# Token mixing on other buffers and engines, and a last norm in another order: one change to a two-block kernel on one core

## The chip, the cores and the metric

The kernel runs on one core of a Trainium2 chip. Its time is the device time of one execution in microseconds (us). Lower is better. The engines are named as in the profile: PE is TensorE (PEld its weight loads), DVE is VectorE, ACT is ScalarE, POOL is GpSimd, SP is SyncE, which issues the DMAs.

## The reference

Two transformer blocks on 256 tokens of width 1024, all in float32. The first has two gated feed-forward layers and, between them, a token mixing layer. The second has attention, a recurrence and a large expert layer, and ends in a layer norm. What the change touches of it:

```python
# token mixing: one projection, two recurrences, one output projection
p = y @ w_in
mq, mk, mv, mo, mif, hq, hf, hi, hg = jnp.split(p, PROJ_IDX, axis=-1)
qk = jax.nn.silu(causal_dwconv(jnp.concatenate([mq, mk], axis=-1), conv_w, conv_b))
hm = merge_heads(mlstm_chunkwise(q, k, v, log_i, log_f))      # gates from mif, values mv
ho = merge_heads(hgrn2_chunkwise(hq_, hk_, hv_, hlf))         # decay from hf, values hi
merged = jnp.concatenate([out_m, out_h], axis=-1).astype(y.dtype)
return merged @ w_out

# the end of the second block
x = _layer_norm(DN_ALPHA * x + _peer(x, ...), ln2_g[l], ln2_b[l])
# _layer_norm: mu = mean(x); var = mean((x - mu)**2); (x - mu) * rsqrt(var + eps) * g + b
```

## The kernel before, in words

Each matrix product is made of three matmuls (`mm3`, lines 276 to 278): weights and activations are split into a high and a low part, and high times high, low times high and high times low are added up. The weights come by DMA from SP's queue, one megabyte or so at a time, into two places that take turns. `split` (lines 264 and 265) makes the high part `wh` on ACT and the low part `wl` on DVE (in some stages on POOL).

A scheduler orders each engine's instructions when the kernel is built, by its own estimates of what is ready when. After that each engine runs its list strictly in order and waits wherever an operand is late. So the lists that it made are what the change is read from.

The mixing layer (`mixer`, from line 558) goes in this order:

- `proj_b` projects the channels that are needed with channels on the partitions (tile `pb`): the decay `hs`, the query `hq`, the convolution's inputs `xq`, and at last the gate rows `gi`.
- `proj_a` projects the values with tokens on the partitions (tile `pa`), in eight steps s of two token halves b, 24 matmuls each: `hv` for s 0 and 1, `mv` for 2 and 3, `hg` for 4 and 5, `mo` for 6 and 7. Each half goes to a PSUM buffer that ACT (or DVE) must empty before it can be written again. The PSUM buffers have three tags: `gu` (2 buffers), `ps` (2) and `acc` (4). `pa` takes `gu`.
- The gate rows (lines 593 to 603) are a chain of small steps on DVE and ACT. PE turns two of the rows (`gm`, line 607) and spreads a third over the partitions (`Mb`, lines 617 to 620), and ACT makes the weights `E` from it.
- The convolution (line 732, 24 steps on DVE) fills `y`, and its sigmoid is three passes of ACT over all of `y` (exp, ln, exp: lines 295 to 297) and one product on DVE (line 735).
- The second recurrence works in nine levels L = 0, 1, 2, 4, ... 128 (lines 655 to 688). A level takes exp of the decay sums `P` and `S` on ACT (lines 662 and 667), multiplies by `hq` and `hk` on DVE (663 and 668), takes products on PE (`lv`, line 678), puts them under a mask into `att` on DVE (680), and, for the next level, widens the sums `S` and `P` (671 and 672).
- Then `S`, `num` (the first recurrence's products, lines 740 to 747) and `ho` (777 and 778) on PE. `num` and `ho` share the tag `acc`. ACT takes squares of both and scales them into `mg` (766 and 784), and `hg` and `mo` multiply that.

The lists of PE put the `pa` matmuls between all these, so that PE has work while it would wait.

The last norm (`finish`) has two token halves b. `centred` adds x and the accumulated `acc` (line 1240, sums on the side), makes minus the mean (1243, 1244), and then the sum of squares: on ACT for b = 0, on DVE for b = 1 (1247). `finish` then scales, a quarter of it on ACT and POOL (1303 to 1305), the rest on DVE (1307, 1308), and SP stores each half row as it is done (1309).

Of the kernel before, what the change touches and what calls it, by code (L numbers as in the profile page):

```python
# [7 lines left out]
F32 = mybir.dt.float32  # L8
# [7 lines left out]
AF = mybir.ActivationFunctionType  # L16
OP = mybir.AluOpType
# [4 lines left out]
D = 1024  # L22
# [150 lines left out]
class K:  # L173
# [368 lines left out]
            for f in fill.get(s, ()):  # L542
                f()

    def proj_a(self, src, s, yh, yl, take):
        w = self.weights(src[s], 2048)
        for b in range(2):
            p = self.psum("pa", tag="gu")
            for k in range(KT):
                wh, wl = w[k // 4]  # L550
                t = slice(b * 128, (b + 1) * 128)
                o = slice((k % 4) * 256, (k % 4) * 256 + 256)
                self.mm3(p[:, :256], yh[:, k, t], yl[:, k, t], wh[:, o], wl[:, o], k == 0, k == KT - 1)
            take(b, p[:, :256])

    def mixer(self, yh, yl, fill):
        nc, A = self.nc, self.A
        act, dve = nc.scalar.activation, nc.vector
        with ExitStack() as ctx:
# [8 lines left out]
            y = mx.tile([128, 8, T], F32, name="y")  # L568
# [23 lines left out]
            m = F  # L592
# [11 lines left out]
            p = self.psum("gm", tag="ps")  # L604
# [9 lines left out]
            for h in range(4):  # L614
                p = self.psum("Mb", tag="ps")
# [25 lines left out]
            hk, P, S = big("hk"), big("P"), big("S")  # L641
            for n in range(4):
                i = slice(n * 256, (n + 1) * 256)
# [11 lines left out]
            for n, L in enumerate((0, 1, 2, 4, 8, 16, 32, 64, 128)):  # L655
                if L == 0:
                    a, b = hq, hk
                else:
                    g = 1024 // (2 * L)
                    half = lambda x, i: x.rearrange("p (g two l) -> p g two l", g=g, two=2)[:, :, i]  # L660
                    a, b = qt[n % 2], kt[n % 2]
                    act(half(a, 1), half(P, 1), AF.Exp)
                    dve.tensor_tensor(half(a, 1), half(a, 1), half(hq, 1), op=OP.mult)
                    if L == 1:
                        b = hk
                    else:
                        act(half(b, 0), half(S, 0), AF.Exp)
                        dve.tensor_tensor(half(b, 0), half(b, 0), half(hk, 0), op=OP.mult)
                    if L < 128:
                        end = lambda i: half(P, i)[:, :, L - 1:L].to_broadcast([128, g, L])  # L670
                        nc.gpsimd.tensor_tensor(half(S, 0), half(S, 0), end(1), op=OP.add)
                        nc.gpsimd.tensor_tensor(half(P, 1), half(P, 1), end(0), op=OP.add)
                if L < 128:
                    for bl in range(2):
                        p = self.psum("lv", tag="ps")
                        for h in range(4):
                            o = h * 256 + bl * 128
                            nc.tensor.matmul(p[:, h * 128:(h + 1) * 128], b[:, o:o + 128], a[:, o:o + 128],
                                             start=True, stop=True)
                        dve.copy_predicated(att[:, bl], lev[:, None, n * 128:(n + 1) * 128].to_broadcast([128, 4, 128]),  # L680
                                            p.rearrange("p (h t) -> p h t", h=4))
                else:
                    p = self.psum("lv", tag="ps")
                    for h in range(4):
                        o = h * 256
                        nc.tensor.matmul(p[:, h * 128:(h + 1) * 128], b[:, o:o + 128], a[:, o + 128:o + 256],
                                         start=True, stop=True)
                    act(cross.rearrange("p h t -> p (h t)"), p, AF.Copy)
# [11 lines left out]
            def values(s):  # L700
                o = (s % 2) * 256

                def take(b, p):
                    if s < 2:
                        act(hv[:, b, o:o + 256], p, AF.Copy)
                    elif s < 4:
                        act(mv[:, b, 2 * (s % 2):2 * (s % 2) + 2, :128], p.rearrange("p (h e) -> p h e", h=2), AF.Copy)
                    elif s < 6:
                        dve.tensor_copy(hg[:, b, o:o + 256], p)
                        act(hgs[:, b, o:o + 256], p, AF.Exp, scale=-1.0)  # L710
                        self.sigmoid_of_exp(hgs[:, b, o:o + 256])
                        t = mg[:, b, 512 + o:768 + o]
                        dve.tensor_tensor(t, t, hg[:, b, o:o + 256], op=OP.mult)
                        dve.tensor_tensor(t, t, hgs[:, b, o:o + 256], op=OP.mult)
                    else:
                        act(mo[:, b, o:o + 256], p, AF.Exp, scale=-1.0)
                        self.sigmoid_of_exp(mo[:, b, o:o + 256])
                        t = mg[:, b, o:o + 256]
                        dve.tensor_tensor(t, t, mo[:, b, o:o + 256], op=OP.mult)

                self.proj_a(A["wina"], s, yh, yl, take)
                for f in fill.get(s, ()):
                    f()

            for s in range(4):
                values(s)
# [4 lines left out]
                for j in range(3):  # L731
                    dve.scalar_tensor_tensor(y[:, n], xq[:, n, j:j + 256], w(j), y[:, n], op0=OP.mult, op1=OP.add)
            ysig = mx.tile([128, 8, 259], F32, name="ysig", tag="xq")[:, :, :T]
            self.sigmoid(ysig, y)
            dve.tensor_tensor(y, y, ysig, op=OP.mult)
            num = [[self.psum(f"num{b}{j}", tag="acc", bufs=4) for j in range(2)] for b in range(2)]
            for h in range(4):
                E = Es[h]
                p = self.psum("S", tag="ps")
# [4 lines left out]
                o = slice((h % 2) * 129, (h % 2) * 129 + 129)  # L744
# [5 lines left out]
            for b in range(2):  # L750
                for j in range(2):
                    v = num[b][j][:, :258].rearrange("p (h e) -> p h e", h=2)
                    act(den[:, 4 * b + 2 * j:4 * b + 2 * j + 2], v[:, :, 128], AF.Abs)
                    for h in range(2):
                        i = 4 * b + 2 * j + h
# [7 lines left out]
            for b in range(2):  # L763
                for h in range(4):
                    o = (h % 2) * 129
                    act(mg[:, b, h * 128:(h + 1) * 128], num[b][h // 2][:, o:o + 128], AF.Copy,
                        scale=fac[:, 4 * b + h:4 * b + h + 1])
# [5 lines left out]
            for b in range(2):  # L773
                for h in range(4):
                    o = ho[b][:, h * 128:(h + 1) * 128]
# [6 lines left out]
            for b in range(2):  # L782
                for h in range(4):
                    act(mg[:, b, 512 + h * 128:640 + h * 128], ho[b][:, h * 128:(h + 1) * 128], AF.Copy,
                        scale=fac[:, 4 * b + h:4 * b + h + 1])

            for s in range(4, 8):
                values(s)
# [501 lines left out]
    def finish(self, wk, acc, out):  # L1290
        dve = self.nc.vector
        g, s = self.row(wk, 2), self.row(wk, 3)
        z = self.work.tile([128, 2, D], F32, name="xn", bufs=1)
        for b in range(2):
            mu, r = self.centred(b, acc, z)
            for h in range(2):
                o = slice(h * 512, (h + 1) * 512)
                x, y = self.x[:, b, o], z[:, b, o]
                if h and not b:

                    m = self.small.tile([128, 1], F32, name="lnm")
                    dve.tensor_tensor(m, mu, r, op=OP.mult)
                    self.nc.scalar.activation(y, y, AF.Identity, scale=r, bias=m)
                    self.nc.gpsimd.tensor_tensor(y, y, g[:, o], op=OP.mult)
                    self.nc.gpsimd.tensor_tensor(x, y, s[:, o], op=OP.add)
                else:
                    dve.scalar_tensor_tensor(y, y, mu, g[:, o], op0=OP.add, op1=OP.mult)
                    dve.scalar_tensor_tensor(x, y, r, s[:, o], op0=OP.mult, op1=OP.add)
                self.nc.sync.dma_start(out[0, b * 128:(b + 1) * 128, o], x)


    def top16(self, pool, val, idx, src, n):
# [374 lines left out]
```

## Time and profile before

| what | value |
|---|---|
| median of 3 runs | 1757.65 us (1756.09 to 1761.62) |
| the profiled execution: its own time, its span | 1756.9 us, 1754.9 us |
| busy share of PE, DVE, ACT, POOL | 96%, 66%, 52%, 17% |
| mean granted TensorE clock | 0.985 of full speed |
| the mixing layer, first `pb` to last `pa` matmul | about 240 to 383 us |
| the last norm, from PE's last matmul to the span's end | 1743 to 1755 us |

The span runs from the first to the last instruction of the trace, and the execution's own time is 2.0 us more. The lists of instructions give start, duration, engine, line, operation and tiles; a bracket at the end is idle time of the engine just before it and what ended that. Matmuls overlap in a pipeline, so their pace is read from start to start, not from their durations. The granted clock is 1.00 at 2.4 GHz and 0.50 at 1.2 GHz; a figure between is a mean over a stretch that has both.

### The profile page before, as it was taken

The numbers are of one execution on the slowest core, as the hardware profiler recorded it, in microseconds if no ns is written. First come the engines' busy times: TensorE is split into PE (matmuls) and PEld (weight loads), VectorE is DVE, ScalarE is ACT, GpSimd is POOL, SyncE is SP. The second block draws the span as 40 slices with busy tenths as digits, with TensorE's granted clock in tenths as the row PEclk, the third lists the DMA queues.
The fourth block names the chain that finished last, engine by engine and source line by source line (L and its number), as shares of the span: only waits on it lengthen the run. The fifth ranks groups of instructions, "written<-read, shape, count | busy, mean of one in ns | idle before, by whom it ended". The sixth has DMA issues, their size and how long they took to land.

```text
span 1754.9 us, 30914 instructions
## 1 busy us (share of the span) xinstructions
PE 1688.1 (96%) x12658; PEld 1536.6 (88%) x12658; DVE 1161.0 (66%) x2057; ACT 910.8 (52%) x1424; POOL 305.7 (17%) x183
## 2 busy tenths in 40 slices
PE   3999999999999998999999999999999999999997
PEld 3899988898999997878889999999888888888886
DVE  8887668778655458344377869998556555655555
ACT  4544376376444457334445445887545444555453
POOL 2000011300000132311005600001322223322321
PEclk8999999999999999999999999999999999999998
DMA  8888433357553231401253567877866666777652
GB/s 326 356 342 332 169 129 113 156 218 312 217 202 130 96 117 53 169 31 63 97 186 132 200 227 251 314 299 294 289 242 244 228 245 218 252 248 257 229 202 84
DMA packets 85677, 362.68 MB, mean 207 GB/s; under 512 B 6432, under 2 KB 39328, under 8 KB 52768
## 3 DMA queue, kind: packets, MB, share of 16 engines
q1 hardware_dynamic: 85536, 360.71, 55.7%
q8 instruction: 99, 1.62, 0.4%
q14 instruction: 42, 0.34, 0.1%
HBM read 333.42 MB, written 27.26 MB: 206 GB/s over the span
## 4 chain that ended last, share of the span: by engine, by line
PE 48%; DVE 10%; issue 1%; DMA 1%; ACT 1%; POOL 0%; DVEq 0%; SPq 0%; ACTq 0%
PE acc L276 7%; PE acc L278 7%; PE acc L277 7%; PE pu L276 5%; PE pu L278 4%; PE pu L277 4%; DVE wl L265 3%; DVE dif L1509 2%; DVE oj L1517 1%; PE pg L276 1%; PE pb L276 1%; PE pb L278 1%; PE pb L277 1%; PE pg L278 1%; PE pg L277 1%
## 5 line engine op out<-in xcount | busy, mean ns | idle before, releaser
L264 ACT ACTIVATE wh<-w 128x1024 fp32r<-128x1024 f32 x402 | 422.6, 1054 | 261.5 <-PE acc L277 110.5
L265 DVE TENSOR_TENSOR wl<-w,wh 128x1024 fp32r<-128x1024 f32 x301 | 371.3, 1238 | 222.1 <-ACT wh L264 216.0
L265 POOL TENSOR_TENSOR wl<-w,wh 128x1024 fp32r<-128x1024 f32 x101 | 246.6, 2442 | 1044.9 <-ACT wh L264 892.0
L276 PE MATMUL pu<-yh,wl 128*128 128x256 f32 x1024 | 292.4, 286 | 0.0
L278 PE MATMUL pu<-yl,wh 128*128 128x256 f32 x1024 | 289.4, 283 | 0.0
L277 PE MATMUL pu<-yh,wh 128*128 128x256 f32 x1024 | 288.6, 282 | 0.0
L276 PE MATMUL acc<-wh,gl 128*128 128x512 f32 x512 | 202.2, 395 | 1.2 <-DVE gl L1609 1.1
L278 PE MATMUL acc<-wl,gh 128*128 128x512 f32 x512 | 202.0, 395 | 0.0
L277 PE MATMUL acc<-wh,gh 128*128 128x512 f32 x512 | 202.0, 395 | 0.0
L277 PEld LDWEIGHTS pu<-yh,wh 128*128 128x128 f32 x1024 | 193.6, 189 | 1.2
L276 PEld LDWEIGHTS pu<-yh,wl 128*128 128x128 f32 x1024 | 193.4, 189 | 1.2
L278 PEld LDWEIGHTS pu<-yl,wh 128*128 128x128 f32 x1024 | 193.1, 189 | 0.0
L278 PE MATMUL gu<-yl,wh 128*128 128x256 f32 x416 | 118.2, 284 | 0.0
L277 PE MATMUL gu<-yh,wh 128*128 128x256 f32 x416 | 117.6, 283 | 0.0
L276 PE MATMUL gu<-yh,wl 128*128 128x256 f32 x416 | 117.4, 282 | 0.0
L276 PEld LDWEIGHTS acc<-wh,gl 128*128 128x128 f32 x512 | 96.4, 188 | 23.2 <-DVE gl L1609 2.1
L278 PEld LDWEIGHTS acc<-wl,gh 128*128 128x128 f32 x512 | 96.5, 188 | 22.6
L277 PEld LDWEIGHTS acc<-wh,gh 128*128 128x128 f32 x512 | 96.4, 188 | 21.4
L276 PE MATMUL pb<-yh,wl 128*128 128x256 f32 (+1 forms) x384 | 110.2, 288 | 0.0
L1605 DVE TENSOR_TENSOR H<-H,gate 128x256 f32<-128x256 f32 x128 | 59.7, 505 | 74.8 <-ACT H L1583 71.6
L278 PE MATMUL pb<-yl,wh 128*128 128x256 f32 (+1 forms) x384 | 108.2, 284 | 0.0
L277 PE MATMUL pb<-yh,wh 128*128 128x256 f32 (+1 forms) x384 | 107.5, 283 | 0.0
(511 smaller groups left out, 3799.6 us busy)
## 6 DMA issues: line engine op xcount, KB each, us to landing
w<-in_pu_dram SPq DMA_DIRECT2D x64, 1024.0 KB, 5.4
w<-in_pv_dram SPq DMA_DIRECT2D x64, 1024.0 KB, 4.9
wx<-in_ffn_dram SPq DMA_DIRECT2D x28, 1536.0 KB, 8.8
wa<-in_ada_dram SPq DMA_DIRECT2D x28, 1024.0 KB, 6.2
w<-in_ffn_dram SPq DMA_DIRECT2D x16, 1536.0 KB, 8.9
gd<-gst SPq DMA_DIRECT2D x8, 2048.0 KB, 8.9
gate<-gd SPq DMA_DIRECT2D x32, 512.0 KB, 6.6
hd<-hs SPq DMA_DIRECT2D x36, 256.0 KB, 5.6
```

Source lines behind the costliest of these rows:

```text
L264: nc.scalar.activation(h[:, :n], w, AF.Copy)
L265: eng.tensor_tensor(l[:, :n], w, h[:, :n], op=OP.subtract)
L276: mm(out, ll, rh, start=first, stop=False, **kw)
L277: mm(out, lh, rh, start=False, stop=False, **kw)
L278: self.mm = mm(out, lh, rl, start=False, stop=last, **kw)
L1509: dve.tensor_tensor(d, ix[:, None, None, :].to_broadcast([128, 2, 8, 64]), ij[:, :, t, None].to_broadcast([128, 2, 8, 64]), op=OP.bitwise_xor)
L1517: self.oj = dve.tensor_tensor(oj.rearrange("p m t j -> p (m t j)").bitcast(U32).rearrange("p (m t j) -> p m t j", m=2, t=8), eq.bitcast(U3 ...
L1605: dve.tensor_tensor(g3, g3, gates[m // 2][:, :, 2 * (m % 2) + i], op=OP.mult)
```

## The change

Four things change. The values of s 0 to 3 go to the tag `acc` with its four buffers. The decay sums (671, 672) are issued on DVE. The convolution's sigmoid and product are made in four pieces of two channel groups. The last norm takes its squares on ACT for both halves, multiplies by the weight row ahead of the deviation into a tile of its own (`yfin`), and leaves POOL out.

```diff
-    def proj_a(self, src, s, yh, yl, take):
+    def proj_a(self, src, s, yh, yl, take, tag="gu"):
         w = self.weights(src[s], 2048)
         for b in range(2):
-            p = self.psum("pa", tag="gu")
+            p = self.psum("pa", tag=tag, bufs=4 if tag == "acc" else 2)
...
                     if L < 128:
                         end = lambda i: half(P, i)[:, :, L - 1:L].to_broadcast([128, g, L])
-                        nc.gpsimd.tensor_tensor(half(S, 0), half(S, 0), end(1), op=OP.add)
-                        nc.gpsimd.tensor_tensor(half(P, 1), half(P, 1), end(0), op=OP.add)
+                        dve.tensor_tensor(half(S, 0), half(S, 0), end(1), op=OP.add)
+                        dve.tensor_tensor(half(P, 1), half(P, 1), end(0), op=OP.add)
...
-                self.proj_a(A["wina"], s, yh, yl, take)
+                self.proj_a(A["wina"], s, yh, yl, take, "acc" if s < 4 else "gu")
...
-            self.sigmoid(ysig, y)
-            dve.tensor_tensor(y, y, ysig, op=OP.mult)
+            for n in range(0, 8, 2):
+                i = slice(n, n + 2)
+                self.sigmoid(ysig[:, i], y[:, i])
+                dve.tensor_tensor(y[:, i], y[:, i], ysig[:, i], op=OP.mult)
...
         z = self.work.tile([128, 2, D], F32, name="xn", bufs=1)
+        y = self.work.tile([128, 2, D], F32, name="yfin", tag="yh", bufs=1)
+        half = lambda h: slice(h * 512, (h + 1) * 512)
         for b in range(2):
-            mu, r = self.centred(b, acc, z)
...
+            self.ss(z[:, b], st[:, 3:4], bias=mu)
+            self.rstd(r, st[:, 3:4], D, self.lneps)
+            for h in range(2):
+                dve.scalar_tensor_tensor(y[:, b, half(h)], z[:, b, half(h)], mu, g[:, half(h)], op0=OP.add, op1=OP.mult)
+            for h in range(2):
+                x = self.x[:, b, half(h)]
+                dve.scalar_tensor_tensor(x, y[:, b, half(h)], r, s[:, half(h)], op0=OP.mult, op1=OP.add)
+                self.nc.sync.dma_start(out[0, b * 128:(b + 1) * 128, half(h)], x)
```

All engines' lists differ in the mixing layer and in the last norm, and nowhere else. Lines after 733 are two higher in the new kernel, those after the last norm five. Three places follow.

DVE, the gate rows' chain from the copy of `gi` to the row that PE turns (line 601), before:

```order
L583 COPY gi<-pb 4x512
L594 TENSOR_SCALAR gi<-gi,cols 4x256
L595 TENSOR_SCALAR gi<-gi,cols 4x256
L596 SCALAR_TENSOR_TENSOR rows<-gi 4x256
L265 TENSOR_TENSOR wl<-w,wh 128x1024
L735 TENSOR_TENSOR y<-y,ysig 128x2048
L599 SCALAR_TENSOR_TENSOR gi<-gi,rows 4x256
L265 TENSOR_TENSOR wl<-w,wh 128x1024
L600 SCALAR_TENSOR_TENSOR rows<-rows,gi 4x256
L265 TENSOR_TENSOR wl<-w,wh 128x1024
L601 TENSOR_TENSOR gi<-gi,rows 4x256
```

The same chain in the new kernel (line 737 was 735):

```order
L583 COPY gi<-pb 4x512
L737 TENSOR_TENSOR y<-y,ysig 128x512
L594 TENSOR_SCALAR gi<-gi,cols 4x256
L595 TENSOR_SCALAR gi<-gi,cols 4x256
L265 TENSOR_TENSOR wl<-w,wh 128x1024
L596 SCALAR_TENSOR_TENSOR rows<-gi 4x256
L737 TENSOR_TENSOR y<-y,ysig 128x512 x2
L599 SCALAR_TENSOR_TENSOR gi<-gi,rows 4x256
L600 SCALAR_TENSOR_TENSOR rows<-rows,gi 4x256
L265 TENSOR_TENSOR wl<-w,wh 128x1024
L601 TENSOR_TENSOR gi<-gi,rows 4x256
```

Three of the four pieces of the product stand in it, and two splits of weights in place of three. On PE's list the first `gm` stands behind 64 `pa` matmuls now, and stood behind 86.

PE, from the third `Mb` block to the first levels, in the new kernel:

```order
L617 MATMUL Mb<-rows,ident 128x256
L618 MATMUL Mb<-upper,ident 128x128
L619 MATMUL Mb<-rows,ident 128x128
L620 MATMUL Mb<-upper,ident 128x128
L678 MATMUL lv<-hq,hk 128x128 x8
L678 MATMUL lv<-qt_2952,hk 128x128 x4
L278 MATMUL pa<-wl,yh 128x256
L276 MATMUL pa<-wh,yl 128x256
L277 MATMUL pa<-wh,yh 128x256
L278 MATMUL pa<-wl,yh 128x256
```

Before, the four `Mb` blocks had 8 `pa` matmuls between them, and 4 stood between the first two levels; now the blocks have 1, and 8 stand in the middle of the second level. From level 8 on, 25 or 26 stand between any two levels, where there were 6 to 14.

DVE, one level's work (L = 16), before:

```order
L663 TENSOR_TENSOR qt_2952<-qt_2952,hq 128x32x16
L668 TENSOR_TENSOR kt_2954<-kt_2954,hk 128x32x16
L680 COPY_PREDICATED att<-lev,lv 128x512
L336 SCALAR_TENSOR_TENSOR wa,mod<-wa,sc 128x1024
L680 COPY_PREDICATED att<-lev,lv 128x512 x2
L663 TENSOR_TENSOR qt_2951<-qt_2951,hq 128x16x32
```

And in the new kernel (`wa` is a column product for a later layer, which moved behind the levels):

```order
L663 TENSOR_TENSOR qt_2952<-qt_2952,hq 128x32x16
L668 TENSOR_TENSOR kt_2954<-kt_2954,hk 128x32x16
L671 TENSOR_TENSOR S<-S,P 128x32x16
L265 TENSOR_TENSOR wl<-w,wh 128x1024
L672 TENSOR_TENSOR P<-P 128x32x16
L680 COPY_PREDICATED att<-lev,lv 128x512 x2
L663 TENSOR_TENSOR qt_2951<-qt_2951,hq 128x16x32
```

The two sums stand in DVE's list, with a split between them, ahead of the copies under the mask.

## Rows read from the trace of the kernel before

**Rows 1.** The page's first part: busy time, share and count of each engine.

```profile
PE 1688.1 (96%) x12658; PEld 1536.6 (88%) x12658; DVE 1161.0 (66%) x2057; ACT 910.8 (52%) x1424; POOL 305.7 (17%) x183
```

**Rows 2.** PE's waits, 240 to 420 us: who for, sum us, times, longest.

```profile
PE pa L276 <- ACT hv L705: 3.4, 1, 3.4
PE lv L678 <- DVE att L680: 2.4, 1, 2.4
...
PE lv L678 <- DVE kt L668: 0.8, 2, 0.5
PE ho L778 <- ACT xn L766: 0.3, 1, 0.3
```

**Rows 3.** Instructions of PE in order, 290 to 304 us: start, duration, what.

```profile
292.00 0.28 PE L276 MATMUL pa<-wh,yl 128*128 128x256 f32 x1
...
297.57 0.28 PE L278 MATMUL pa<-wl,yh 128*128 128x256 f32 x1
301.20 0.39 PE L276 MATMUL pa<-wh,yl 128*128 128x256 f32 x1 [3.35 <-ACT hv L705]
...
303.12 0.41 PE L277 MATMUL pa<-wh,yh 128*128 128x256 f32 x1
303.33 0.41 PE L278 MATMUL pa<-wl,yh 128*128 128x256 f32 x1
```

**Rows 4.** Instructions of ACT in order, 290 to 306 us.

```profile
293.65 1.92 ACT L295 ACTIVATE ysig<-y 128x2048 f32<-128x2048 f32 x1 [4.84 <-DVE y L732]
...
300.80 0.36 ACT L705 ACTIVATE hv<-pa 128x256 f32<-128x256 f32 x1
```

**Rows 5.** Instructions of DVE in order, 290 to 308 us.

```profile
293.48 0.67 DVE L583 COPY gi<-pb 4x512 f32<-4x512 f32 x1
...
298.51 1.22 DVE L265 TENSOR_TENSOR wl<-w,wh 128x1024 fp32r<-128x1024 f32 x1 [3.27 <-ACT wh L264]
...
306.02 0.41 DVE L601 TENSOR_TENSOR gi<-gi,rows 4x256 f32<-4x256 f32 x1
```

**Rows 6.** Instructions of PE in order, 310 to 342 us.

```profile
312.75 0.69 PE L617 MATMUL Mb<-rows,ident 4*128 4x256 f32 x2
...
314.86 0.76 PE L617 MATMUL Mb<-rows,ident 4*128 4x256 f32 x2
...
317.59 3.62 PE L678 MATMUL lv<-hq,hk 128*128 128x128 f32 x16
...
338.71 2.02 PE L678 MATMUL lv<-qt,kt 128*128 128x128 f32 x16 [0.53 <-DVE kt L668]
```

**Rows 7.** A stretch: PE, PEld, DVE, ACT, POOL busy, granted clock, DMA share, GB/s.

```profile
315.00:320.00 5.00, 5.00 (x20) 4.15 (x21) 2.74 (x4) 1.47 (x5) 0.11 (x1) 0.54 0.17 69
```

**Rows 8.** Instructions of DVE in order, 330 to 344 us.

```profile
331.29 0.69 DVE L663 TENSOR_TENSOR qt<-qt,hq 128x512 f32<-128x512 f32 x1
331.90 0.69 DVE L668 TENSOR_TENSOR kt<-kt,hk 128x512 f32<-128x512 f32 x1
...
341.40 2.08 DVE L265 TENSOR_TENSOR wl<-w,wh 128x1024 fp32r<-128x1024 f32 x1
```

**Rows 9.** Line 672: engine, count, minimum/median/maximum ns, first and last start.

```profile
L672 POOL TENSOR_TENSOR P<-P x7: 1366/1708/1972, 262.6 to 342.5; 128x512 f32<-128x512 f32 x7
```

**Rows 10.** Instructions of DVE and ACT in order, last norm.

```profile
1741.43 0.16 DVE L1243 TENSOR_TENSOR lnst<-lnst 128x1 f32<-128x1 f32 x1
...
1741.82 1.15 ACT L366 ACTIVATE junk<-xn,lnst 128x1024 bf16<-128x1024 f32 x1 [11.38 <-DVE lnst L1244]
...
1743.42 0.20 ACT L308 ACTIVATE lnst<-lnst 128x1 f32<-128x1 f32 x1
...
1745.41 1.22 DVE L1243 TENSOR_TENSOR lnst<-lnst 128x1 f32<-128x1 f32 x1
...
1746.85 2.18 DVE L1247 SCALAR_TENSOR_TENSOR junkv<-xn,lnst 128x1024 f32<-128x1024 f32 x1
...
1750.40 1.41 DVE L1308 SCALAR_TENSOR_TENSOR x<-xn,lnst,row 128x512 f32<-128x512 f32 x2
```

More of the change, by code (lines that the diff above doesn't have):

```diff
@@ L1293, in finish @@
         z = self.work.tile([128, 2, D], F32, name="xn", bufs=1)
+        y = self.work.tile([128, 2, D], F32, name="yfin", tag="yh", bufs=1)
+        half = lambda h: slice(h * 512, (h + 1) * 512)
         for b in range(2):
-            mu, r = self.centred(b, acc, z)
+            st = self.small.tile([128, 5], F32, name="lnst")
             for h in range(2):
[L1297 to L1309, printed above, removed]
+                dve.scalar_tensor_tensor(z[:, b, half(h)], self.x[:, b, half(h)], 2.0 ** 0.25, acc[b][h], op0=OP.mult,
+                                         op1=OP.add, accum_out=st[:, h:h + 1])
+            mu, r = st[:, 2:3], st[:, 4:5]
+            dve.tensor_tensor(mu, st[:, 0:1], st[:, 1:2], op=OP.add)
+            i = dve.tensor_scalar(mu, mu, -1.0 / D, None, op0=OP.mult)
+            self.ss(z[:, b], st[:, 3:4], bias=mu)
[6 more added lines that the diff above has]
+                self.nc.sync.dma_start(out[0, b * 128:(b + 1) * 128, half(h)], x)
     def top16(self, pool, val, idx, src, n):
```

## The prediction

> **What bounds the kernel now.** The page's first part comes first: PE is busy for 96% of the span, the next engine for 66% [rows 1]. PE's matmuls do not change, so the change can only take out time in which PE waits or runs slowly, and the end behind PE's last matmul. All of that is small: 1% is 17.6 us.
>
> Next come PE's own waits in the mixing layer. Four kinds bear on the change, 6.9 us in all: 3.4 for the eviction of `hv`, 2.4 for a copy under the mask, 0.8 for `kt`, 0.3 for the scaling ahead of `ho` [rows 2].
>
> PE's list around the longest wait shows what it costs. The first 48 `pa` matmuls start 0.119 us apart (292.00 to 297.57 is 47 steps), then PE stands for 3.35 us, and behind it matmuls start 0.21 apart [rows 3]. That is the pace of the lower granted clock, 1.2 GHz. The neighbouring list of ACT says why PE stood: ACT was in the convolution's sigmoid, three passes of 1.92 us, and came to `hv` at 300.80 [rows 4]. Both `gu` buffers were full until then.
>
> A second slow stretch has no wait in front of it. From 315 to 320 us PE is busy all the time, at a granted clock of 0.54 [rows 7]. Ahead of it lie the `Mb` blocks. The first level's sixteen `lv` records span 3.62 us there, against 2.02 at full clock, and a block of `Mb` goes from 2.11 us (two `pa` among it) to 2.73 [rows 6].
>
> The last view is the end of the trace. There DVE alone sets the time: it takes a step of 0.16 us in 1.22 while POOL works, and the squares of b = 1 in 2.18 [rows 10].
>
> **The change part by part.**
>
> *Values in four buffers, sigmoid in pieces.* Removed: the wait of 3.35 us, and the slow pace behind it, some 15 steps of 0.213 - 0.119, 1.4 us [rows 3]. Together 4.75. In the new order PE goes through 64 `pa` matmuls before it needs anything else, from 292.0 to 299.6. Then it needs the gate row of line 601, which came at 306.4 before [rows 5]. So the next late thing is that chain. Its rows by the new list, from a copy of `gi` at about 293: the copy 0.67, three pieces of the product at 0.61 (a product of that size starts 0.61 before the next [rows 8]), four small steps at 0.41, a scan at about 0.6, two splits at 1.22 [rows 5], line 601 itself 0.41: 7.6 us, so 300.6. The 3.27 us that DVE stood behind the split of weights, itself behind ACT's long passes, go away: ACT was idle for 4.84 us before its first pass because the whole of `y` had to be ready [rows 4], and a piece needs only two of the eight groups. I take a wait of 1.0. Its bounds: 0, where the chain is as quick as PE's 64 matmuls, and 6.8, where it comes no earlier than before. Term: -4.75 + 1.0 = -3.75.
>
> ACT's pieces cost it more. From 0.36 us for 256 columns and 1.92 for 2048 [rows 4], 512 columns are about 0.58, twelve of them 7.0 against 5.8. This lies in the 4.84 idle, and if that cover were gone the 1.2 us would go onto the chain, inside the bound above.
>
> *The slow stretch at `Mb`.* Before, it cost 0.86 in the last block (2.73 against 2.11 less two `pa`), 1.6 in the first level, and 0.4 in four `pa`: 2.8 us [rows 3, 6]. The new order packs the blocks closer, one `pa` between them in place of eight, and puts one and a half levels behind them before the next `pa`. I take 1.6 for the first level, 1.2 for most of the second, 0.75 for eight `pa`: 3.6. Term: +0.8. Bounds: -2.8, where the clock stays up, and about +5, where it stays down until the third level has ended.
>
> *Decay sums on DVE.* Removed: the waits at the levels, 2.4 + 0.8 = 3.2 us [rows 2]. The 2.4 came from a split of weights that took 2.08 us in place of 1.22, while POOL was in a sum [rows 5, 8]. Added: nine sums on DVE behind 292 us, five ahead of it. No row has such a sum on DVE. The nearest is the product of the same size, 0.61 from start to start; the far end is POOL's own 1.71 [rows 8, 9]. I take 0.61, since it is the same engine and shape. A level is then, in DVE's list, two products, two sums, two copies under the mask at about 0.61 and a split at 1.22: 4.9 us. PE has 25 `pa` and one level of about 1.9 to do in that time, with the change from one to the other about 5.15. So PE stays behind DVE, barely, and the waits shrink to some 0.5 in all. Term: -2.7. Bounds: -3.2, and up to about +7 with sums at POOL's price (rival C).
>
> The trace has a split beside POOL's work at 2.08 us, and alone at 1.22 [rows 5, 8]: 0.86 lost for one of POOL's sums. The Trainium skill, Perfetto Trace Analysis, section on optimizing Scalar/DVE operations, warns that DVE and GpSimd share a read port, so moving work between the two might not help. Read that way, DVE would pay 0.61 for what it lost before, and the term would be near 0 and the sum 2.7 worse; I keep the term, because PE's waits at the levels came from few such clashes.
>
> *Between the levels and the end of the layer.* Here the order gives back a little. With 46 more `pa` done by then, the first recurrence's `num` comes sooner behind DVE's products with `E`: about 0.5 of waiting. `ho` needs a buffer that `num` leaves once ACT has scaled it, and the squares ahead of that now share ACT with two splits and pieces of `hg`: I take a wait of 1.3 where it was 0.3 [rows 2]. Term: +1.5. Bounds: 0 to +3.
>
> *The last norm.* From 1741.82, when ACT starts the squares of b = 0, DVE has six passes of 512 columns: two products by the weight row, the sum of the first half of b = 1, two last steps of b = 0, the sum of the second half. At 0.70 each (1.41 for two) that is 1746.0; two small steps, 0.4 (1741.43 to 1741.82), 1746.4; ACT's squares and the deviation, 1.8 (1741.82 to 1743.62), 1748.2, with the next two products beside them; two last steps 1.4: 1749.6. Before, the last step ended at 1751.81 [rows 10]. Term: -2.2. Bounds: -2.6 and -1.2, as DVE meets the square later or sooner; the store at the end is the same.
>
> The sum: -3.75 + 0.8 - 2.7 + 1.5 - 2.2 = -6.35 us. From the profiled execution's 1756.9 that is 1750.55. The median of the runs lies 0.75 above that execution, so the forecast for a median is **1751.3**, with its own range of 1749 to 1754.
>
> **The rivals.**
>
> *A, the clock stays up.* PE's slow pace behind the wait goes with the wait, and if the slow stretch at `Mb` is a late effect of the same wait, it goes too. For it: both lie in one stretch of 25 us, and elsewhere the clock is mostly whole. Against it: from 305 to 315 the pace was whole again, and no wait comes before 315 [rows 2, 7]. Worth 0.8 + 2.8: 1747.7. The Trainium skill, TensorE: Matmul & The Clock Gate, on the clock gate, has the clock fall after idling and rise with activity. The first fall agrees with that, the second, with PE busy 5.00 of 5.00, does not.
>
> *B, the wait moves to the gate rows.* DVE has the sums as well now, and the chain stands behind splits that wait for DMA and ACT. If it comes at 303.6, PE waits 4.0 in place of 1.0: 1754.3. For it: every one of its steps waits for another engine or stands in a full list. Against it: the 3.27 idle is gone in any reading.
>
> *C, DVE becomes the bound in the levels: slower.* If a sum costs DVE what it costs POOL, 1.71, a level is 7.1 us against PE's 5.15, and five levels lose 9.75; the five early sums put 5.5 onto the gate rows' chain. 1751.3 + 15.25 is about 1766. The point where the change gains nothing: 15 times the extra per sum, less the 1.25 of slack, is 6.35, at 1.1 us a sum. Against it: the same engine does a product of that shape in 0.69.
>
> *D, only the last norm gains.* PE saves its waits early, meets `num`, `ho` or the clock instead, and the layer ends when it did: 1757.65 - 2.2 = 1755.5. For it: two thirds of the sum rest on waits that come and go with the order.
>
> **How the numbers follow.** 0.3% is 5.3 us, about what a measurement of this kernel can tell from no change, so faster means below 1752.4. The forecast has 0.52 (0.42 below that line, 0.10 above), A 0.14, B 0.16, D 0.11, C 0.07. Faster is 0.42 + 0.14 = 0.56, the same 0.10 + 0.16 + 0.11 = 0.37, slower 0.07. The range of 1746.5 to 1756.5 takes in A, B and D with about 1 us around them and leaves out C and the far ends of the bounds.
>
> **What would show it.** In the new profile `pa` no longer waits for `hv`, and the product of line 737 starts before 295. The first `gm` starts at 300 to 301; a start past 303 is rival B. The granted clock between 306 and 320 decides between A and the forecast. The sums on DVE (lines 671, 672) have a median near 0.69; at 1.1 or more the forecast is wrong. `lv` waits sum to under 1 us. The first `ho` starts near 362, and the last `pa` near 378 in place of 383; 382 is rival D. In the last norm the squares of b = 1 stand on ACT at 1.15, no small step of DVE takes over 0.3, and the last step ends some 6.3 us after PE's last matmul (1743.3 before) in place of 8.5.

## The result, and the profile after

The changed kernel takes **1739.17 us** (median of 6 runs, 1736.62 to 1740.86) against 1759.63 for the kernel before: a ratio of 0.9882, 95% interval 0.9868 to 0.9895. Faster was forecast, but 1751.3 was the forecast and 1746.5 the lower end. The gain is three times the one forecast.

The profiled execution spans 1738.9 us, 16.0 less than before; it was the slowest of its six runs, so the traces show less than the medians. The starts of the same instructions in the two traces show where it comes from. A third column is experiment e1 below, the changed kernel with the SBUF addresses of the kernel before.

| start, us | before | after | e1 |
|---|---|---|---|
| first `gu` (first feed-forward layer) | 52.08 | 51.87 | 51.94 |
| first `pb` (mixing layer) | 239.87 | 237.95 | 239.75 |
| first `pa` | 292.00 | 288.91 | 291.55 |
| last `pa` of the layer | 382.51 | 375.19 | 375.96 |
| `sq` (start of the second block's recurrence) | 652.56 | 642.90 | 646.10 |
| first `pu` (expert layer) | 980.88 | 970.25 | 976.04 |
| last `acc` | 1743.06 | 1729.43 | 1738.84 |
| end of the span | 1754.9 | 1738.9 | 1748.3 |

Between the last `pa` and `sq` neither kernel has another list, and yet the changed one gains 2.3 us more there; in e1 the distance to before changes by 0.1. It gains 1.7 on the way from the first `gu` to the first `pb`, ahead of every edit.

The groups of PE's matmuls by line and shape (busy time, mean ns of one) say what is quicker. Before:

```profile
L276 PE MATMUL pu<-yh,wl 128*128 128x256 f32 x1024 | 292.4, 286 | 0.0
L277 PE MATMUL gu<-yh,wh 128*128 128x256 f32 x416 | 117.6, 283 | 0.0
L277 PE MATMUL gu<-yh,whx 128*128 128x256 f32 x240 | 67.8, 282 | 0.0
```

After:

```profile
L276 PE MATMUL pu<-yh,wl 128*128 128x256 f32 x1024 | 289.7, 283 | 0.0
L277 PE MATMUL gu<-yh,wh 128*128 128x256 f32 x416 | 116.3, 280 | 0.0
L277 PE MATMUL gu<-yh,whx 128*128 128x256 f32 x240 | 67.9, 283 | 0.0
```

The same matmul takes 3 ns less where `yh` streams against `wh` or `wl`, and nothing less where it streams against `whx`, a second place for split weights in the feed-forward layers. How many matmuls fit into a stretch without waits, in the first feed-forward layer, says the same. The columns are those of [rows 7]; the first bracket counts PE's matmuls. Before:

```profile
60.00:160.00 100.00, 100.00 (x700) 93.66 (x699) 82.29 (x123) 45.02 (x60) 0.00 (x0) 1.00 0.85 336
```

After:

```profile
60.00:160.00 100.00, 100.00 (x710) 93.63 (x709) 83.15 (x125) 45.73 (x60) 0.00 (x0) 1.00 0.84 335
```

Ten matmuls more in 100 us, at full clock, with PE busy throughout in both.

Where the change was made, the profile after answers like this. PE's waits from 240 to 420 us, in place of [rows 2]:

```profile
PE gm L607 <- issue: 1.7, 1, 1.7
PE tp L436 <- DVE diag L375: 1.2, 1, 1.2
```

The waits for `hv`, the levels and `ho` are gone, 6.9 us, and one for the gate row (`gm`) has come. "issue" means that the profile names no engine for it; the row comes from DVE's line 601, which ends at 298.22. PE's list shows the wait, and behind it the `Mb` blocks and the first level at half pace, where [rows 6] had one block and the level so:

```profile
296.36 0.28 PE L276 MATMUL pa<-wh,yl 128*128 128x256 f32 x1
298.32 0.25 PE L607 MATMUL gm<-ident,gi 4*128 4x4 f32 x2 [1.68 <-issue]
...
310.43 1.22 PE L617 MATMUL Mb<-rows,ident 4*128 4x256 f32 x2
...
313.61 3.62 PE L678 MATMUL lv<-hq,hk 128*128 128x128 f32 x16
```

The granted clock of that stretch, as [rows 7]:

```profile
302.00:316.00 14.00, 14.00 (x44) 10.00 (x44) 0.61 (x2) 3.14 (x9) 0.11 (x1) 0.50 0.35 148
```

The sums of line 672 on DVE, in place of [rows 9]:

```profile
L672 DVE TENSOR_TENSOR P<-P x7: 666/686/704, 259.5 to 342.2; 128x512 f32<-128x512 f32 x7
```

And the last norm's end on DVE, in place of [rows 10]; PE's last matmul ends at 1729.83:

```profile
1732.16 0.16 DVE L1304 TENSOR_TENSOR lnst<-lnst 128x1 f32<-128x1 f32 x1
...
1732.55 1.42 DVE L1310 SCALAR_TENSOR_TENSOR yfin<-xn,lnst,row 128x512 f32<-128x512 f32 x2
1734.38 1.42 DVE L1313 SCALAR_TENSOR_TENSOR x<-yfin,lnst,row 128x512 f32<-128x512 f32 x2 [0.42 <-ACT lnst L308]
```

No small step takes 1.22 us any more, and the last one ends 6.0 us behind PE (1735.80 less 1729.83), against 8.4 before.

### The profile page after: what moved, and what is told of

Read it like the earlier page. It is cut to its first block, busy times and chain, and to the rows that moved or that the text cites. A ratio compares the mean times of both kernels' runs of the same rounds, so it can differ in the third digit from the quotient of the medians.

```text
span 1738.9 us, 30896 instructions
## 1 busy us (share of the span) xinstructions
PE 1680.8 (97%) x12658; PEld 1526.3 (88%) x12658; DVE 1161.8 (67%) x2073; ACT 912.6 (52%) x1434; POOL 283.2 (16%) x167
## 4 chain that ended last, share of the span: by engine, by line
PE 82%; DVE 12%; ACT 3%; DMA 2%; issue 2%; POOL 0%; SPq 0%; DVEq 0%; ACTq 0%; POOLq 0%
PE acc L276 10%; PE acc L277 10%; PE acc L278 10%; PE pu L276 5%; PE pu L277 5%; PE pu L278 5%; PE gu L276 4%; PE gu L277 4%; PE gu L278 4%; DVE wl L265 3%; PE pb L276 2%; PE pb L278 2%; PE pb L277 2%; DVE dif L1514 1%; PE pg L276 1%
```

## The experiments

The old last norm had a small tile `lnm`, in three slots of 32 bytes per partition. The new one has none. The tiles are laid out one after the other, so every tile behind these slots starts 96 bytes lower in the changed kernel: `yh` and `yl` at 114272 and 106080 in place of 114368 and 106176, and `whx` with them. `wh` and `wl` lie ahead of the slots and did not move. That is the one difference that reaches the untouched layers. Ratios below are to the kernel before, timed on the same chip.

**e1: the old addresses back.**

```diff
+        self.small.tile([128, 24], F32, name="pad", bufs=1)     # never read or written
```

> The changed kernel with 96 unused bytes per partition put back where the old last norm had its three slots of lnm, so that every tile behind them, yh and yl among them, has its old SBUF address; every engine's list is that of the changed kernel. Theory 1 (addresses): TensorE's pace in the layers that the change does not touch depends on where yh and yl lie against wh and wl; then pu<-yh,wl has a mean of about 286 ns again (283 in the changed kernel), and the time is some 9 to 14 us above the changed kernel's 1739.2: 1748 to 1753. Rival (the pace is a matter of the execution or the chip, or comes from the new order): 283 ns stays and the time is 1737 to 1741.

Measured: 1749.84 us, ratio 0.9941 (0.9928 to 0.9953). The group of `pu` in line 276:

```profile
L276 PE MATMUL pu<-yh,wl 128*128 128x256 f32 x1024 | 293.2, 286 | 0.0
```

The stretch of the first feed-forward layer:

```profile
60.00:160.00 100.00, 100.00 (x700) 93.64 (x699) 82.25 (x123) 44.87 (x60) 0.00 (x0) 1.00 0.84 335
```

286 ns and 700 matmuls again. With an order that is not touched, 96 unused bytes cost 10.7 us by the medians. In the mixing layer PE's waits, 240 to 420 us, are these:

```profile
PE tp L436 <- DVE diag L375: 1.2, 1, 1.2
PE gm L607 <- issue: 1.1, 1, 1.1
```

**e2: the new addresses for the kernel before.**

```diff
-        st = self.small.tile([128, 5], F32, name="lnst")
+        st = self.small.tile([128, 6], F32, name="lnst")
...
-        return mu, r
+        self.lm = st[:, 5:6]; return mu, r
...
-                    m = self.small.tile([128, 1], F32, name="lnm")
+                    m = self.lm
```

> The kernel before with lnm kept in a free column of lnst, so that 96 bytes per partition go and every tile behind them has the address that it has in the changed kernel; every engine's list is that of the kernel before. Theory 1 (addresses): pu<-yh,wl falls from 286 to 283 ns and the time from 1759.6 to 1746 to 1751. Rival (execution, chip or order): 286 ns and 1757 to 1762.

Measured: 1750.21 us, ratio 0.9942 (0.9930 to 0.9955). The same group:

```profile
L276 PE MATMUL pu<-yh,wl 128*128 128x256 f32 x1024 | 289.7, 283 | 0.0
```

And the same stretch:

```profile
60.00:160.00 100.00, 100.00 (x710) 93.60 (x709) 83.18 (x125) 45.78 (x60) 0.00 (x0) 1.00 0.85 335
```

The kernel before gains 0.58% by the bytes alone. Half of the result comes from the places of tiles, which moved because the new last norm has no `lnm`, and not from what the four edits do.

**e3 and e4: other distances.** The changed kernel with less padding than e1.

```diff
+e3:     self.small.tile([128, 8], F32, name="pad", bufs=1)
+e4:     self.small.tile([128, 16], F32, name="pad", bufs=1)
```

> The changed kernel with 32 unused bytes: yh, yl and what lies behind them are 64 bytes below their old address, in place of 96. Theory 1a (what counts is whether moving and stationary operand start at the same place modulo 64 bytes): like e1, 1748 to 1753. Theory 1b (modulo 128 bytes): like the changed kernel, 1737 to 1741. Rival (addresses do not matter): 1737 to 1741 here and in e1.

> The changed kernel with 64 unused bytes: yh, yl and what lies behind them are 32 bytes below their old address. Theories 1a and 1b both give the changed kernel's time, 1737 to 1741, since the operands no longer start at the same place modulo 64 or 128 bytes. A time at 1748 or more would mean that it is not the residue but the particular address of 96 bytes below that is quick.

Measured: e3 1739.93 us (0.9887, 0.9873 to 0.9901), e4 1752.61 us (0.9964, 0.9950 to 0.9977). A place 64 bytes lower is as quick as one 96 lower, one 32 lower is no quicker than the old one. So 1a falls with e3, and 1b with e4. From 60 to 160 us PE made 706 matmuls in e3 and 699 in e4, against 710 at the new addresses and 700 at the old. The mean of one is a weaker sign: `pu<-yh,wl` has 284 ns in e4, near the quick 283, in a slow kernel.

**e11: 32 bytes higher.** The last two lines stand ahead of the feed-forward layers' own tiles.

```diff
+        self.small.tile([128, 32], F32, name="pad", bufs=1)
+                wk.tile([128, 8], F32, name="pad1")
+                wk.tile([128, 16], F32, name="pad2")
```

> The changed kernel with 128 unused bytes, so that yh and yl lie 32 bytes above their old address; in the first feed-forward layer whx lies another 32 bytes higher, in the second another 64. Theory with a period of 128 bytes (96 below equals 32 above, 64 below equals 64 above): pu<-yh,wl at 283 ns and the time 1737 to 1741; gu<-yl,whx, 32 below in one layer and 64 below in the other, in between. Rival (no such period, small shifts in either direction are slow): 284 to 286 ns, 1748 to 1753.

Measured: 1741.84 us (0.9907, 0.9892 to 0.9921), `pu<-yh,wl` at 285 ns. In between: near the quick ones, short of the forecast. The stages disagree. The first feed-forward layer is the quickest of all, with 712 matmuls from 60 to 160 us, but there `whx` has another distance too. The expert layer takes 761.8 us from the first `pu` to the last `acc`, as at the old addresses (762.2 before, 759.2 in the changed kernel). No rule by a residue follows from these five places.

**e13 and e14: relative or own place.**

```diff
e13: e2, and ahead of the buffers w, wh and wl:
+        self.st.tile([128, 24], F32, name="pad")
e14: the kernel before, and ahead of all tiles:
+        c.tile([128, 40], F32, name="pad")
```

> The kernel before with lnm in a free column of lnst (96 bytes less) and 96 unused bytes ahead of the buffers w, wh and wl: these lie 96 bytes higher, and yh, yl and all behind them at their old addresses; every engine's list is that of the kernel before. Theory R (the place of yh and yl relative to wh and wl counts): as in e2, pu<-yh,wh at 280 ns and 1748 to 1752. Theory P (the own place of yh and yl counts): as the kernel before, 282 to 283 ns and 1757 to 1762.

> The kernel before with 160 unused bytes ahead of everything that TensorE reads for its large products: x, w, wh, wl, yh, yl and the rest lie 160 bytes higher, at the same distances as before. Theory R (relative place): as the kernel before, pu<-yh,wh at 282 to 283 ns and 1757 to 1762. Theory P (own place; 160 higher is the same as 96 lower modulo 32, 64, 128 and 256 bytes): as in e2, 280 ns and 1748 to 1752.

Measured: e13 1747.29 us (0.9929, 0.9913 to 0.9944), e14 1758.61 us (0.9990, 0.9980 to 0.9999). The group of line 277 in e13:

```profile
L277 PE MATMUL pu<-yh,wh 128*128 128x256 f32 x1024 | 285.8, 279 | 0.0
```

In e14:

```profile
L277 PE MATMUL pu<-yh,wh 128*128 128x256 f32 x1024 | 289.9, 283 | 0.0
```

Moving the weights does the same as moving `yh`, within the intervals; moving both does nothing over 0.2%. So for `yh` and `yl` against `wh` and `wl` it is the distance between the streamed operand and the loaded weights that counts, and neither one's own place.

**e10: the second place of weights.** e9 below, with padding ahead of `whx` in both feed-forward layers, so that its distance to `yh` becomes one that was quick for `wh`.

```diff
+                wk.tile([128, 24], F32, name="pad1")
+                wk.tile([128, 24], F32, name="pad2")
```

> As e9, and in the two feed-forward layers the extra places for split weights (whx, wlx) lie 96 bytes higher, at their old addresses again, while yh and yl stay at the new ones. Theory (the place of the moving operand relative to the stationary one counts): the products gu<-yh,whx, which kept 283 ns in every kernel so far because both moved together, fall to 279 or 280; 720 of them start some 3 ns earlier each: 2 us less than e9, 1733 to 1735. Rival (the absolute address of the weights or of yh counts): 283 ns stays, no change against e9.

Measured: 1735.90 us (0.9871, 0.9855 to 0.9888); e9 had 0.9887.

```profile
L277 PE MATMUL gu<-yh,wh 128*128 128x256 f32 x416 | 116.5, 280 | 0.0
L277 PE MATMUL gu<-yh,whx 128*128 128x256 f32 x240 | 67.6, 281 | 0.0
```

The group that had stayed at 282 or 283 wherever `whx` moved with `yh` falls by 2 ns, as the relative theory has it. But its neighbours, whose distances are as in e9, rise by up to 2 (`gu<-yh,wl` from 279 to 281), which that theory does not explain, and the feed-forward layer ends no earlier. The expected 2 us lie inside the intervals and don't show in the layer.

**e5: the four banks alone.**

```diff
-            p = self.psum("pa", tag="gu")
+            p = self.psum("pa", tag=tag, bufs=4 if tag == "acc" else 2)
...
-                self.proj_a(A["wina"], s, yh, yl, take)
+                self.proj_a(A["wina"], s, yh, yl, take, "acc" if s < 4 else "gu")
```

> The kernel before with one edit: the values of s 0 to 3 take the tag acc with its four buffers. Every engine's list and every SBUF address is that of the kernel before; only the PSUM buffers differ. Theory (the wait moves, rival B of the prediction in its pure form): the wait of 3.4 us for hv goes, but the gate row of line 601 still comes at about 306.4 in the old order, so that PE now waits for it, about 3.4 + 1.4 us less the slow pace that follows any wait: net gain 0 to 1.5 us, 1757.7 to 1759.3. Rival (the wait for hv was the whole loss): 3.4 + 1.4 = 4.8 us gained, 1754.4.

Measured: 1761.57 us, ratio 1.0010 (1.0000 to 1.0019). PE's waits:

```profile
PE gm L607 <- issue: 4.0, 1, 4.0
PE lv L678 <- DVE att L680: 2.4, 1, 2.4
```

The wait of 3.4 for `hv` became one of 4.0 for the gate row, and the `Mb` blocks behind it took 12.4 us (their steps from start to start added up, without the `pa` between them), where they took 7.9. The wait moved as rival B has it, and even the 0 to 1.5 us expected did not come.

**e6: banks and pieces of the sigmoid.** As e5, and:

```diff
-            self.sigmoid(ysig, y)
-            dve.tensor_tensor(y, y, ysig, op=OP.mult)
+            for n in range(0, 8, 2):
+                i = slice(n, n + 2)
+                self.sigmoid(ysig[:, i], y[:, i])
+                dve.tensor_tensor(y[:, i], y[:, i], ysig[:, i], op=OP.mult)
```

> The kernel before with the four banks and the sigmoid in pieces, decay sums and last norm as before, old SBUF addresses. Theory: the gate rows' chain comes sooner with the pieces, so PE waits 1.0 to 1.7 us for gm in place of 3.4 for hv, the slow pace behind hv goes (1.4), and the Mb blocks, closer to each other, lose up to 3 us more to the lower granted clock: net gain 1 to 4 us, 1755 to 1758. Rival (the mixing layer's gain in e1, about 6 us, is all from here): 1753.

Measured: 1764.80 us, ratio 1.0033 (1.0021 to 1.0046): slower. PE's waits:

```profile
PE gm L607 <- issue: 4.1, 1, 4.1
PE lv L678 <- DVE kt L668: 2.3, 2, 1.2
```

The stretch of the `Mb` blocks:

```profile
306.00:324.00 18.00, 18.00 (x55) 12.47 (x55) 1.26 (x4) 3.41 (x10) 0.11 (x1) 0.50 0.35 147
```

The same stretch before:

```profile
306.00:324.00 18.00, 18.00 (x98) 14.95 (x97) 8.50 (x14) 5.77 (x13) 0.11 (x1) 0.81 0.55 227
```

PE waits as long as in e5, and then does all four `Mb` blocks, now packed, at 1.2 GHz. The chain did come forward, by 2.9 us; this is DVE's line 601, which [rows 5] have at 306.02:

```profile
303.11 0.40 DVE L601 TENSOR_TENSOR gi<-gi,rows 4x256 f32<-4x256 f32 x1
```

But PE comes to it sooner still, without the wait for `hv` and with 63 `pa` records ahead of it in place of 86. And the chain takes 10.2 us from the copy of `gi` (293.29) to the end of line 601, where the prediction had 7.6: its first product starts at 296.22, behind a convolution that ends as late as before.

**e7: the decay sums alone.**

```diff
-                        nc.gpsimd.tensor_tensor(half(S, 0), half(S, 0), end(1), op=OP.add)
-                        nc.gpsimd.tensor_tensor(half(P, 1), half(P, 1), end(0), op=OP.add)
+                        dve.tensor_tensor(half(S, 0), half(S, 0), end(1), op=OP.add)
+                        dve.tensor_tensor(half(P, 1), half(P, 1), end(0), op=OP.add)
```

> The kernel before with one edit: the decay sums on DVE, old SBUF addresses. Theory: the waits at the levels (3.3 us) go to under 0.5, as DVE's split of weights no longer shares with POOL's sums; the time falls by about 3 us to 1756. Rival 1 (the waits go only because the other edits put more pa matmuls between the levels): 0 to 1 us, 1758 to 1759. Rival 2 (a sum costs DVE over 1.1 us): slower, 1760 or more. The sums' median on DVE is 0.6 to 0.7 us by the theory.

Measured: 1751.71 us, ratio 0.9954 (0.9940 to 0.9968): the most of any edit tried alone at the old addresses, and more than any theory had. PE's waits, 240 to 420 us:

```profile
PE tp L436 <- DVE diag L375: 1.2, 1, 1.2
PE pa L276 <- ACT hv L705: 0.4, 1, 0.4
PE gm L607 <- DVE gi L601: 0.4, 1, 0.4
```

The levels' waits are gone without any other edit, and so is nearly all of the wait for `hv`, which had been put down to the two buffers. The cause lies some 25 to 35 us earlier, in two places. The first is ACT, which waited for POOL's second sum and did its later steps, evictions of `pb` among them, that much later. Before, and then in e7:

```profile
264.50 0.69 ACT L662 ACTIVATE qt<-P 128x512 f32<-128x512 f32 x1 [2.33 <-POOL P L672]
...
262.36 0.68 ACT L662 ACTIVATE qt<-P 128x512 f32<-128x512 f32 x1 [0.29 <-DVE P L672]
```

DVE's first product of line 663 starts at 268.53 in e7, 1.48 us sooner than before (270.01). The second place is DVE itself, at 271 us, where POOL's next three sums run from 271.52 to 276.36. Before, with the first of them:

```profile
271.52 1.71 POOL L671 TENSOR_TENSOR S<-S,P 128x512 f32<-128x512 f32 x1 [0.80 <-ACT kt L667]
...
271.75 2.02 DVE L663 TENSOR_TENSOR qt<-qt,hq 128x512 f32<-128x512 f32 x1
273.69 1.53 DVE L668 TENSOR_TENSOR kt<-kt,hk 128x512 f32<-128x512 f32 x1
275.14 1.50 DVE L732 SCALAR_TENSOR_TENSOR y<-xq,cols,y 128x256 f32<-128x256 f32 x1
```

The same place in e7:

```profile
270.27 0.69 DVE L663 TENSOR_TENSOR qt<-qt,hq 128x512 f32<-128x512 f32 x1
270.87 0.69 DVE L668 TENSOR_TENSOR kt<-kt,hk 128x512 f32<-128x512 f32 x1
271.47 0.69 DVE L671 TENSOR_TENSOR S<-S,P 128x512 f32<-128x512 f32 x1
```

Two products and a sum take 1.8 us where two products took 3.4. From there on the whole chain is some 3.2 us earlier. ACT's list in e7, against [rows 4]:

```profile
290.49 1.92 ACT L295 ACTIVATE ysig<-y 128x2048 f32<-128x2048 f32 x1 [2.33 <-DVE y L732]
...
297.63 0.36 ACT L705 ACTIVATE hv<-pa 128x256 f32<-128x256 f32 x1
```

The sigmoid starts 3.16 us sooner, `hv` is emptied 3.17 sooner, and the wait of 3.35 is 0.45.

**e8: the last norm alone,** with e1's padding.

```diff
...
-                    dve.scalar_tensor_tensor(y, y, mu, g[:, o], op0=OP.add, op1=OP.mult)
...
+                dve.scalar_tensor_tensor(y[:, b, half(h)], z[:, b, half(h)], mu, g[:, half(h)], op0=OP.add, op1=OP.mult)
...
```

> The kernel before with the new last norm alone, and 96 unused bytes so that all SBUF addresses stay those of the kernel before. Theory: from PE's last matmul to the end of the span 9.1 us in place of 11.45, and nothing else differs: 1759.3 - 2.4 = 1756.9. Rival (the gain beyond the mixing layer came with this edit in some other way): 1750 to 1753.

Measured: 1755.98 us, ratio 0.9977 (0.9966 to 0.9988). From PE's last matmul to the end 9.1 us, as in the changed kernel, 11.45 before.

**e9: decay sums and last norm,** the edits of e7 and e8 without padding, so at the new addresses; banks and sigmoid as before.

> The kernel before with the decay sums on DVE and the new last norm, which has no lnm (so the SBUF addresses are those of the changed kernel); values in two buffers and the sigmoid whole, as before. Theory: the four buffers and the pieces take back some 3 us of what the decay sums give (mixing layer 81.4 us in e7, 84.4 in e1), so this kernel is 2 to 4 us quicker than the changed one: 1735 to 1737. Rival (with the decay sums in place, buffers and pieces help or are neutral): 1739 or more.

Measured: 1737.77 us, ratio 0.9887 (0.9868 to 0.9905). The changed kernel has 0.9882. Beside the sums, banks and pieces neither help nor cost anything that can be measured, and the theory that they take back 3 us finds no support. It came from two traces, which could not tell it: the time from the first to the last `pa` was 81.2 to 86.3 us in five kernels with one and the same list (the changed kernel, e1, e3, e4, e11). The shortest, e4, has 6.8 us at the lower clock there, the longest, the changed kernel, 17.1. The parts add up: 0.46% (e7), 0.23% (e8) and 0.58% (e2) are 1.27%, against 1.13% in e9 and 1.18% in the changed kernel, within the intervals.

**e12: the mask products in bf16,** on top of e10.

```diff
-                nc.tensor.matmul(p[:, 0:128], self.ident, self.upper, start=False, stop=True)
+                nc.tensor.matmul(p[:, 0:128], self.identb, self.upperb, start=False, stop=True)
... (and the same for columns 256 to 384)
```

> As e10, and the eight products ident by upper in the Mb blocks (fp32, about 0.4 us each at the full clock, 0.73 at the lower) take bf16 copies of both, which hold 0, 1 and 1e30 well enough for the mask. Theory: 8 times 0.3 at the full clock to 8 times 0.65 at the lower, 2.4 to 5 us less than e10: 1729 to 1732. Rival (the lower clock then falls on the levels or on pa in place of the Mb blocks, or PE waits for E): under 1 us.

Measured: 1734.71 us, ratio 0.9856 (0.9840 to 0.9872), the lowest of all. The `Mb` blocks take 6.8 us in place of 8.5 in e10, start to start; 1.6 us less, under the theory's lower end. Its lead over e10 lies inside the intervals, so the rival, under 1 us, is not excluded. The version with the sums, the norm, the new distances and the bf16 mask, without banks and pieces, is 1.4% quicker than the kernel before; its interval reaches just into that of the changed kernel (0.9868 to 0.9895).

## Why the prediction was wrong

The step that failed stands in its first paragraph: "PE's matmuls do not change, so the change can only take out time in which PE waits or runs slowly, and the end behind PE's last matmul." Their number does not change, nor their order outside the mixing layer, but their pace does: `lnm` goes, `yh` comes 96 bytes nearer to `wh`, and the 256-column products that stream it take 2 to 3 ns less. That is 0.58% in e2, 0.71% in e13, and 0.59% between e1 and the changed kernel, 10 to 12 us. No term held it, and the range did not reach it.

What the steps did cover is the difference between the kernel before and e1, where the addresses are the same: 9.4 us by the medians, 6.6 in the two profiled spans, against 6.35. By the spans the sum came out near, by the medians a third short, and that it came so near is luck in part, since its terms are in the wrong places:

- *Values and sigmoid, -3.75.* What was forecast for PE came true at the old addresses: in e1 the wait for `hv` is gone, and the first `gm` starts at 300.43 with a wait of 1.1 (300 to 301 and 1.0 were forecast). But these two edits do not earn it. Without the sums on DVE they cost 0.33% (e6), with the gate rows' chain 4 us late, as rival B has it; beside the sums they do nothing that can be measured (e9). The sums on DVE brought the copy of `gi` 1.5 us forward (291.75 in e1, 293.29 in e6) and the chain behind it down from 10.2 to 8.6 us. The forecast had a copy at 293 and a chain of 7.6; the two errors cancel.
- *The slow stretch at `Mb`, +0.8.* The direction held, the size did not: the blocks take 10.6 us in e1 and 12.7 in the changed kernel, 7.9 before. The granted clock was 0.50 from 302 to 316 in the changed kernel, so rival A is out.
- *Decay sums, -2.7.* The mis-sized term. The waits at the levels went as forecast, 3.2 us, and a sum costs DVE 0.69 us, so rival C is out. But the five early sums were entered only as a cost to DVE. The trace of before had rows of DVE work stretched from 0.69 to 2.02 us beside them, upstream of the wait for `hv`, and a wait of ACT of 2.33 us for one of the sums; the wait for `hv` was followed back to ACT's sigmoid and no further. Alone the edit is worth 0.46%, 8 us. (Rival C counts 15 sums; lines 671 and 672 make 14, which moves its point of no gain to 1.15 us.)
- The Trainium skill, SBUF — State Buffer, section on SBUF's two separate sides, has DVE and GpSimd hold a shared pair of ports for a whole instruction, the other standing still. The rows agree: 2.02 us is the 0.69 of the product and most of the 1.71 of POOL's sum. The prediction's worry that such a move might not help is answered by e7, which is quicker.
- *Between levels and end, +1.5.* Not seen: no wait for `num`, and none for `ho`.
- *The last norm, -2.2.* Right: 11.45 us became 9.07, that is 2.4.

Of what the prediction asked of the profile nearly all came true: no wait for `hv`, no waits at the levels, the sums at 0.69, the last step of the norm 6.0 us after PE's last matmul. The three starts that it gave came 2 to 3 us early: `gm` at 298.32, `ho` at 359.98, the last `pa` at 375.19. A prediction whose signs are nearly all confirmed can still miss half of the effect, if that half has no sign in its list. The one that was missing: stages that the change does not touch take the same time.

## What to carry to other kernels

Compare the untouched stages first, by the count of matmuls in a stretch without waits; when they differ, hold the addresses fixed with padding before any edit is given the credit. A tile that goes or comes moves all that lie behind it, so an allocation is part of every change. And follow a wait upstream past the engine that ends it: the work that made it late may have been stretched by a third engine, 25 us earlier.

## What the runs showed of the hardware

In this kernel the pace of the matmuls that stream `yh` and `yl` (256 columns) depends on their distance in SBUF from the weights that are loaded. With `yh` and `yl` moved by 0, -32, -64, -96 and +32 bytes against `wh` and `wl`, the changed kernel took 1749.84, 1752.61, 1739.93, 1739.17 and 1741.84 us (in the last, `whx` has another distance too). The same 96 bytes did next to nothing where the roles are swapped or the stream is longer: the first 48 `pa`, which stream `wh` against `yh`, start 0.119 us apart before and 0.118 after, and of 512 columns `acc<-wh,gl` took 395 ns before and 396 after. What in the memory makes the distances differ is open; so is whether it repeats with some number of bytes.

The granted clock fell to its lower level behind PE's waits of 3.4 and 4 us, which was expected, and also in e7, some 7 us behind the second of two waits of 0.4, in a stretch of `Mb` blocks with PE busy. Whether the waits or the kind of matmul brings it down was not separated.
